# A Trainium2 encoder: the second mixer's key and query projections made pair by pair, and GpSimd scaling the softmax rows of three head pairs

## The chip, the cores and the metric

One core of a Trainium2 chip. The metric is the device time of one execution in microseconds (us), the median of several runs. TensorE is PE in the profile, VectorE DVE, ScalarE ACT, GpSimd POOL and SyncE SP.

## The reference

Two sequences of 256 tokens with 1024 channels go through two layers. Each layer is a mixer and a convolutional feed-forward, both with a residual sum and a layer norm. The first mixer is neighbourhood attention with a gated unit; the second, which the change touches, is latent attention beside a convolution branch:

```
h = x @ w_in;  c_q, c_kv, k_r, glu_a, glu_g = split(h)
q = rmsnorm(c_q) @ w_uq        # 8 heads, 64 plain + 32 rotary channels
k, v = split(rmsnorm(c_kv) @ w_ukv)
p = softmax((q . k) * 96 ** -0.5);  c = p @ v
d = glu_a * sigmoid(glu_g)
d = silu(layernorm(dwconv31(d)))
m = concat([c, d]) @ w_out
x = layernorm(ALPHA * x + m)
```

## The kernel before

All data are fp32. A large product is made of three matmuls on reduced-precision halves: a weight comes by DMA as `raw`, ACT rounds it to `whi` (L109), DVE makes the rest `wlo` (L111); activations are split in the same way (`split`, L114). PE runs 128x512 matmuls of these (`mm`, L95).

The second mixer (`odd_mixer`, L532) handles 512 tokens at once, eight heads as four pairs. `glu(i)` makes one quarter of the convolution branch's input: two products `glu` with `xT`, then a Sigmoid on ACT (L551), a product on DVE into `dpad`, and the start of that quarter's 31-tap convolution. The 21 first taps run on DVE, summing in PSUM (`cacc`, L719); the ten others are products on ACT (`pr`, L723) that GpSimd sums into `acc` (L724). They run beside the attention. `cproj` and `chain` make the normalized latents `cT`. `kvproj` makes V and the keys `kT` of all pairs, and `qproj` the queries `qT` of all pairs, both ahead of `glu(2)`.

`attend(p)` calls `attention` (L480) for a pair: for each sequence the scores of both heads go to PSUM banks `s` (two buffers), DVE takes the row maximum (L491), ACT the exponentials with their sums (L494) into a tile `er`, DVE the inverse sums `ri` (L497). Then the rows are scaled by `ri`: on ACT (L501, two instructions of 128x256) in pairs 0 to 2, on DVE (L503) in pair 3. PE transposes the result into `pt` (L508), ACT copies it to `PTr` (L510), and PE multiplies it with V (`pv`), which is split into `mixT`. The tiles `er` are a fixed ring of four. The output projection `op` (banks `op` and `dn`) takes `mixT` of the attention and then of the convolution; `conv_ln` (L727) norms the latter. GpSimd adapts the old residual (`affine`, L191). `ToFeat.done` (L228) norms a block of 128 tokens, PE transposes it (`lnT`, L237), ACT and DVE split it into the `xT` of the feed-forward (L246 to L249), whose products are `up`.

A scheduler sets the order in which each engine's instructions stand: it moves work between these steps by priorities and by its own estimate of times, so that the matmuls of `glu(2)` and `glu(3)`, say, stand among those of the attention. Semaphores hold each instruction until its operands are there and its buffer is free.

Of the kernel before, what the change touches and what calls it, by code (L numbers as in the profile page):

```python
# [11 lines left out]
AF = mybir.ActivationFunctionType  # L12
ALU = mybir.AluOpType
AX = mybir.AxisListType

P = 128
D = 1024
KC = 8
S = 256
T = 512  # L20
# [29 lines left out]
def tile_encoder(ctx: ExitStack, tc: tile.TileContext, I, O):  # L50
    nc = tc.nc
# [7 lines left out]
    pB = ctx.enter_context(tc.tile_pool(name="pB", bufs=2, space=bass.MemoryType.PSUM))  # L59
    pC = ctx.enter_context(tc.tile_pool(name="pC", bufs=2, space=bass.MemoryType.PSUM))  # L60
# [7 lines left out]
    def act(shape, dt=F32, s="a"):  # L68
        return actp.tile(shape, dt, tag="act", name=nm(s))

    def tmp(shape, dt=F32, s="t"):
        return tp.tile(shape, dt, tag="tmp", name=nm(s))
# [4 lines left out]
    class Ring:  # L77
# [6 lines left out]
        def get(self):  # L84
            j = self.i % (2 * len(self.t))
            self.i += 1
            return self.t[j // 2][:, j % 2, :].rearrange("p (a k) -> p a k", a=2)

    def bank(pool, s="ps"):
        return pool.tile([P, 512], F32, tag="b", name=nm(s))  # L90

    last_mm = [None]

    def mm(out, lhsT, rhs, first, last):
        last_mm[0] = nc.tensor.matmul(out=out, lhsT=lhsT, rhs=rhs, start=first, stop=last)  # L95
# [384 lines left out]
    def attention(p, score, V, mix, post, er, PTr, on_act=False, last_pair=False):  # L480
        for s in range(2):
            PT = [PTr.get(), PTr.get()]
            pss = [bank(pB, "s").rearrange("p (a k) -> p a k", a=2) for _ in range(2)]
            for qt in range(2):
                score([pss[h][:, qt, :] for h in range(2)], slice(s * S + qt * P, s * S + qt * P + P),
                      slice(s * S, s * S + S))
            for h in range(2):
                e = er.get()
                sc = post(pss[h], h, e)
                nmx = small(2, "nmx")  # L490
                nc.vector.tensor_reduce(out=nmx, in_=sc, axis=AX.X, op=ALU.max, negate=True)  # L491
                rs = small(2, "rs")
                for qt in range(2):
                    nc.scalar.activation(out=e[:, qt, :], in_=sc[:, qt, :], func=AF.Exp,  # L494
                                         bias=nmx[:, qt:qt + 1], accum_out=rs[:, qt:qt + 1])
                ri = small(2, "ri")
                nc.vector.reciprocal(out=ri, in_=rs)  # L497
                last_ri[0] = ri[:, 0:1]
                for qt in range(2):
                    if on_act:  # L500
                        nc.scalar.activation(out=e[:, qt, :], in_=e[:, qt, :], func=AF.Copy, scale=ri[:, qt:qt + 1])  # L501
                    else:
                        nc.vector.tensor_scalar(out=e[:, qt, :], in0=e[:, qt, :], scalar1=ri[:, qt:qt + 1],  # L503
                                                scalar2=None, op0=ALU.mult)
                pt = bank(pC, "pt")
                for kc in range(2):
                    for qt in range(2):
                        nc.tensor.transpose(pt[:, (2 * kc + qt) * P:(2 * kc + qt + 1) * P],  # L508
                                            e[:, qt, kc * P:(kc + 1) * P], ident)
                (nc.vector.tensor_copy if last_pair else nc.scalar.copy)(  # L510
                    out=PT[h], in_=pt.rearrange("p (k q) -> p k q", k=2))

            def pv_stage(s=s, PT=PT):
                pv = bank(pC, "pv")
                for kc in range(2):
                    for h in range(2):
                        mm(pv[h * 64:(h + 1) * 64, :S], V[s][:, kc, (2 * p + h) * 64:(2 * p + h + 1) * 64],
                           PT[h][:, kc, :], kc == 0, kc == 1)
                split(mix, pv[:, :S], slice(s * S, s * S + S))
            flush_pv()  # L520
            pend.append(pv_stage)
# [10 lines left out]
    def odd_mixer(xT):  # L532
# [37 lines left out]
        pr_ring = Ring(1, "pr")  # L570
        rope = const.tile([P, 2, 2, 32], F32, name="rope")
        after_mm(nc.gpsimd.dma_start(out=rope, in_=I["rope"]), last_mm[0])
        G = {"start": last_mm[0]}

        def cproj():
            psc = dn_banks()
            wc = [wload(I["wc"][:, 2 * k2:2 * k2 + 2, :].rearrange("p k n -> p (k n)"), 832) for k2 in range(4)]
            G["wkv"] = wload(I["wukv"], 1024)
            G["wq"] = [wload(I["wuq"][:, k, :], 1024) for k in range(2)]
            for s in range(2):  # L580
                for k in range(KC):
                    o = (k % 2) * 416
                    for t in (2 * s, 2 * s + 1):
                        gemm_tok([psc[t]], xT[k], t, *wc[k // 2], [slice(o, o + 416)], k == 0, k == KC - 1)
            G["psc"] = psc

        def chain():
            cT = G["cT"] = [act([P, 2, T], F32R, "cT") for _ in range(3)]
            G["kr"] = act([P, 2, T], s="kr")
            krT, ropeT = G["kr"][:, 0, :], G["kr"][:, 1, 0:S]  # L590
# [43 lines left out]
                                                                in1=cT[i][:, 0, :].bitcast(F32), op0=ALU.mult,  # L634
                                                                op1=ALU.subtract)

        def qproj():
            cT = G["cT"]
            wq = G["wq"]
            ropeT = G["kr"][:, 1:2, 0:S].broadcast_to([P, 2, S])  # L640
            qT = G["qT"] = [act([P, 2, T], s="qT") for _ in range(4)]

            def qfeat(pool, c):
                ps = bank(pool, "q")
                for k in range(2):
                    wh, wl = wq[k][0][:, c * P:(c + 1) * P], wq[k][1][:, c * P:(c + 1) * P]
                    mm(ps, wh, cT[k][:, 0, :], k == 0, False)
                    mm(ps, wh, cT[k][:, 1, :], False, False)
                    mm(ps, wl, cT[k][:, 0, :], False, k == 1)
                return ps  # L650
            for p in range(4):
                ps = qfeat(pB, 4 + p)
                for h in (0, 1):
                    rows = slice(64 - 64 * h, 128 - 64 * h)
                    nc.vector.tensor_tensor(out=qT[p][rows, h, :].rearrange("p (s t) -> p s t", s=2),  # L655
                                            in0=ps[rows].rearrange("p (s t) -> p s t", s=2), in1=ropeT[rows],
                                            op=ALU.mult)
                ps = qfeat(pC, p)
                for h in (0, 1):
                    rows = slice(64 * h, 64 * h + 64)  # L660
                    nc.scalar.activation(out=qT[p][rows, h, :], in_=ps[rows], func=AF.Copy, scale=96 ** -0.5)

        def kvproj():
            cT = G["cT"]
            wkv = G["wkv"]
            V = G["V"] = [wp.tile([P, 2, 512], F32, tag="w", name=nm("V1")) for _ in range(2)]
            for t in range(NT):
                ps = bank(pB, "v1")
                gemm_tok([ps], cT[2], t, wkv[0], wkv[1], [slice(512, 1024)], True, True)
                nc.scalar.copy(out=V[t // 2][:, t % 2, :], in_=ps)  # L670
            kT = G["kT"]
            for p in range(4):
                ps = bank(pC, "k1")
                wh, wl = wkv[0][:, p * P:(p + 1) * P], wkv[1][:, p * P:(p + 1) * P]
                mm(ps, wh, cT[2][:, 0, :], True, False)
                mm(ps, wh, cT[2][:, 1, :], False, False)
                mm(ps, wl, cT[2][:, 0, :], False, True)
                for h in range(2):
                    rows = slice(64 * h, 64 * h + 64)
                    nc.scalar.copy(out=kT[p][rows, h, :], in_=ps[rows])  # L680

        def attend(p):
            if p == 0:
                G["ring"] = Ring(2, "er"), Ring(2, "PTr")
            er, PTr = G["ring"]
            qT, kT = G["qT"][p], G["kT"][p]

            def score(out, qs, ks):
                for h in range(2):
                    mm(out[h], qT[:, h, qs], kT[:, h, ks], True, True)  # L690
            mixT[p] = act([P, 2, T], F32R, "mixT")
            if p == 2:
                G["sink"] = ToFeat(xscr[1], 1, last_mm[0], "ln1_g1", "ln1_b1", xscr[2], ())
            attention(p, score, G["V"], mixT[p], lambda ps, h, e: ps, er, PTr, p < 3, p == 3)
# [4 lines left out]
        cproj()  # L699
        chain()  # L700
        glu(1)
        kvproj()
        qproj()
        glu(2)
        attend(0)
        attend(1)
        glu(3)
        op = OutProj("wout1", mixT, [0, 1, 2, 3], [4, 5, 6, 7])
# [6 lines left out]
        for i in range(4):  # L715
            a, a2 = accps[i].rearrange("p (s t) -> p s t", s=2), acc2[i // 2][:, i % 2]
            for j in range(1, 31 - NPOOL):
                with tc.issue_after(G["cT_lo"].ins) if i == 0 and j >= 18 else nullcontext():
                    nc.vector.scalar_tensor_tensor(out=a, in0=dpad[i][:, :, j:j + S], scalar=pc("cw", i * 32 + j),  # L719
                                                   in1=a, op0=ALU.mult, op1=ALU.add)  # L720
# [201 lines left out]
```

## Time and profile before

| | us |
|---|---|
| runs | 1105.21, 1104.36, 1104.05 (median 1104.36) |
| the profiled execution | 1104.76 |
| its span | 1102.9 |
| PE busy in the span | 1082.3 (98%) |
| DVE, ACT, GpSimd busy | 673.2, 488.7, 226.6 |
| chain that ended last, share of PE | 93% |

Busy time is the time in which at least one instruction of the engine ran; an idle engine costs only where PE waits for it. The second mixer stands from about 560 to 740 us of the span.

### The profile page before, as it was taken

The page shows a single profiled execution, that of the slowest core. Times are in us where ns is not written, and L with a number is a line of the kernel's source. Part 1 is how long each engine was busy: PE and PEld are TensorE (multiplying, and loading weights), DVE is VectorE, ACT ScalarE, POOL GpSimd, SP SyncE. Part 2 cuts the span into 40 slices and gives each one's busy share as a digit, 9 for nine tenths or more (in the row PEclk, how much of TensorE's full clock was granted, in tenths as well). Part 3 has the DMA queues.
Part 4 walks back from the last instruction along what each step waited for, and adds up shares of the span by engine and source line. Part 5 has one row for each costly group of instructions (what it writes and reads, how often), then busy time and mean ns, then how long its engine had stood idle before and what let it go on. Part 6 is the DMA issues. An engine that isn't in the chain of part 4 may idle for free.

```text
span 1102.9 us, 13655 instructions
## 1 busy us (share of the span) xinstructions
PE 1082.3 (98%) x5210; PEld 900.8 (82%) x5210; DVE 673.2 (61%) x996; ACT 488.7 (44%) x783; POOL 226.6 (21%) x222
## 2 busy tenths in 40 slices
PE   9999999999999999999999979999999999999996
PEld 7888778988888888888898856899888888888885
DVE  5378955766565656422578999587665656542227
ACT  5436644544444444421266797355444444431110
POOL 0482001200000000005464661830000000000173
PEclk9999999999999999999999979999999999999999
DMA  7852223533333323645232104254333333222602
GB/s 256 244 141 77 60 103 107 163 105 96 96 96 96 96 96 99 206 166 180 80 122 58 38 20 153 66 172 122 100 96 96 96 96 96 96 96 96 215 34 76
DMA packets 36098, 124.21 MB, mean 113 GB/s; under 512 B 4289, under 2 KB 5057, under 8 KB 36033
## 3 DMA queue, kind: packets, MB, share of 16 engines
q1 hardware_dynamic: 28864, 100.05, 29.5%
q0 software_dynamic: 6448, 22.53, 6.0%
q8 instruction: 41, 0.67, 0.3%
q10 hardware_dynamic: 720, 0.75, 0.2%
q14 instruction: 25, 0.20, 0.1%
HBM read 113.88 MB, written 8.39 MB: 111 GB/s over the span
## 4 chain that ended last, share of the span: by engine, by line
PE 93%; DVE 3%; ACT 2%; issue 1%; DMA 0%; POOL 0%; POOLq 0%; DVEq 0%; ACTq 0%
PE up L95 44%; PE dn L95 29%; PE qk L95 4%; PE op L95 4%; PE glu L95 3%; PE v L95 2%; PE u L95 2%; PE s L95 1%; PE pv L95 1%; PE pt L508 1%; DVE cacc L719 1%; PE lnT L237 1%; DVE wlo L111 1%; DVE qT L655 0%; ACT er L494 0%
## 5 line engine op out<-in xcount | busy, mean ns | idle before, releaser
L95 PE MATMUL up<-xT,whi 128*128 128x512 f32 (+1 forms) x1536 | 439.9, 371 | 0.0
L111 DVE TENSOR_TENSOR wlo<-raw,whi 128x1024 fp32r<-128x1024 f32 (+1 forms) x174 | 238.8, 1374 | 297.4 <-ACT whi L109 296.1
L95 PEld LDWEIGHTS up<-xT,whi 128*128 128x128 f32 x1536 | 279.9, 188 | 49.9
L109 ACT CAST whi<-raw 128x1024 fp32r<-128x1024 f32 (+1 forms) x174 | 182.4, 1050 | 249.1 <-PE dn L95 132.6
L95 PE MATMUL up<-xT,wlo 128*128 128x512 f32 (+1 forms) x768 | 284.0, 372 | 0.0
L95 PE MATMUL dn<-whi,gT 128*128 128x512 f32 x704 | 217.4, 389 | 0.0
L95 PEld LDWEIGHTS up<-xT,wlo 128*128 128x128 f32 x768 | 144.4, 188 | 24.9
L95 PEld LDWEIGHTS dn<-whi,gT 128*128 128x128 f32 x704 | 132.0, 188 | 27.2
L95 PE MATMUL dn<-wlo,gT 128*128 128x512 f32 x352 | 136.9, 389 | 0.0
L186 POOL DMA_DIRECT2D xres<-xscr x12 | 6.5, 546 | 576.0 <-PE dn L95 576.0
L95 PEld LDWEIGHTS dn<-wlo,gT 128*128 128x128 f32 x352 | 66.1, 188 | 13.8
L115 ACT CAST gT<-cv 128x512 fp32r<-128x512 f32 x44 | 27.3, 620 | 111.6 <-DVE cv L782 111.6
L771 ACT ACTIVATE cv<-up,par 128x512 f32<-128x512 f32 x88 | 68.3, 776 | 0.0
L774 DVE SCALAR_TENSOR_TENSOR cv<-up,par,cv 128x510 f32<-128x510 f32 x88 | 65.8, 748 | 2.7
L781 ACT ACTIVATE cv<-cv 128x512 f32<-128x512 f32 x44 | 27.8, 632 | 85.2 <-DVE cv L774 85.2
L772 DVE SCALAR_TENSOR_TENSOR cv<-up,par,cv 128x510 f32<-128x510 f32 x88 | 65.4, 743 | 0.0
L719 DVE SCALAR_TENSOR_TENSOR cacc<-dpad,par,cacc 128x512 f32<-128x512 f32 x80 | 58.9, 750 | 1.1
L724 POOL TENSOR_TENSOR acc<-acc,pr 128x512 f32<-128x512 f32 x36 | 48.7, 1353 | 38.9 <-ACT pr L723 32.2
L116 DVE TENSOR_TENSOR gT<-cv,gT 128x512 fp32r<-128x512 f32 x44 | 30.4, 692 | 27.5 <-ACT gT L115 27.5
L95 PE MATMUL op<-whi,mixT 128*128 128x512 f32 x128 | 44.3, 402 | 0.0
L95 PE MATMUL dn<-whi,mixT 128*128 128x512 f32 x128 | 42.8, 394 | 0.0
L95 PE MATMUL glu<-xT,khi 128*128 128x512 f32 (+1 forms) x160 | 42.0, 349 | 0.0
(195 smaller groups left out, 1351.4 us busy)
## 6 DMA issues: line engine op xcount, KB each, us to landing
raw<-in_wup SPq DMA_DIRECT2D x88, 512.0 KB, 3.6
raw<-in_wdn SPq DMA_DIRECT2D x44, 512.0 KB, 3.5
raw<-in_wout SPq DMA_DIRECT2D x16, 512.0 KB, 3.7
xscr<-xres POOLq DMA_DIRECT2D x12, 512.0 KB, 3.7
xres<-xscr POOLq DMA_DIRECT2D x12, 512.0 KB, 4.4
raw<-in_wqk SPq DMA_DIRECT2D x8, 512.0 KB, 6.6
raw<-in_wglu SPq DMA_DIRECT2D x8, 512.0 KB, 3.8
raw<-in_wug SPq DMA_DIRECT2D x7, 512.0 KB, 3.6
```

The source lines that it names most:

```text
L95: last_mm[0] = nc.tensor.matmul(out=out, lhsT=lhsT, rhs=rhs, start=first, stop=last)
L109: nc.scalar.copy(out=hi[:, :n], in_=raw[:, :n])
L111: nc.vector.tensor_tensor(out=lo[:, :n], in0=raw[:, :n], in1=hi[:, :n].bitcast(F32), op=ALU.subtract)
L115: nc.scalar.copy(out=dst[:, 0, sl], in_=src)
L116: nc.vector.tensor_tensor(out=dst[:, 1, sl], in0=src, in1=dst[:, 0, sl].bitcast(F32), op=ALU.subtract)
L237: nc.tensor.transpose(self.banks[k // 2][:, (k % 2) * S + q * P:(k % 2) * S + q * P + P], x[:, k * P:(k + 1) * P], ident)
L719: nc.vector.scalar_tensor_tensor(out=a, in0=dpad[i][:, :, j:j + S], scalar=pc("cw", i * 32 + j), in1=a, op0=ALU.mult, op1=ALU.add)
L724: nc.gpsimd.tensor_tensor(out=a2, in0=a2, in1=pr, op=ALU.add)
L771: nc.scalar.activation(out=c, in_=pv, func=AF.Identity, scale=pc(fw, ch * 4 + 1), bias=pc(fw, ch * 4 + 3))
L772: nc.vector.scalar_tensor_tensor(out=c[:, :, 1:S], in0=pv[:, :, 0:S - 1], scalar=pc(fw, ch * 4), in1=c[:, :, 1:S], op0=ALU.mult, op1=ALU.add)
L774: nc.vector.scalar_tensor_tensor(out=c[:, :, 0:S - 1], in0=pv[:, :, 1:S], scalar=pc(fw, ch * 4 + 2), in1=c[:, :, 0:S - 1], op0=ALU.mult, o ...
L781: nc.scalar.activation(out=cg, in_=cg, func=AF.Silu)
```

## The change

`kvproj` and `qproj` become `kqproj(p)`, which makes the key, the rotary and the plain query of one pair, and `vproj`. Pairs 0 and 1 and V are made ahead of `glu(2)`, pairs 2 and 3 after `attend(0)`. In pairs 0 to 2 one GpSimd instruction of 128x512 multiplies a head's rows by `ri`, repeated along the row, in place of ACT's two. The tile `e` now comes from the pool of temporaries (eight buffers, shared with the Sigmoid's and other tiles). Lines of code move by four.

```diff
--- before.py
+++ after.py
@@ -85,6 +85,10 @@
+
+    class Loose:
+        def get(self):
+            return tmp([P, 512], s="e").rearrange("p (a k) -> p a k", a=2)
@@ -496,10 +500,10 @@
                 ri = small(2, "ri")
                 nc.vector.reciprocal(out=ri, in_=rs)
                 last_ri[0] = ri[:, 0:1]
+                if on_act:
+                    nc.gpsimd.tensor_tensor(out=e, in0=e, in1=ri[:, :, None].broadcast_to([P, 2, S]), op=ALU.mult)
                 for qt in range(2):
-                    if on_act:
-                        nc.scalar.activation(out=e[:, qt, :], in_=e[:, qt, :], func=AF.Copy, scale=ri[:, qt:qt + 1])
-                    else:
+                    if not on_act:
                         nc.vector.tensor_scalar(out=e[:, qt, :], in0=e[:, qt, :], scalar1=ri[:, qt:qt + 1],
                                                 scalar2=None, op0=ALU.mult)
@@ -634,55 +638,51 @@
+        def kqproj(p):
+            cT, wkv, kT = G["cT"], G["wkv"], G["kT"][p]
...
+            qT = G["qT"][p] = act([P, 2, T], s="qT")
+            ps = bank(pC, "k1")
...
+            for h in range(2):
+                rows = slice(64 * h, 64 * h + 64)
+                nc.scalar.copy(out=kT[rows, h, :], in_=ps[rows])
+            ps = qfeat(pB, 4 + p)
...
+            ps = qfeat(pC, p)
...
+        def vproj():
...
         def attend(p):
             if p == 0:
-                G["ring"] = Ring(2, "er"), Ring(2, "PTr")
-            er, PTr = G["ring"]
+                G["ring"] = Ring(2, "PTr")
+            er, PTr = Loose(), G["ring"]
@@ -699,10 +699,13 @@
         glu(1)
-        kvproj()
-        qproj()
+        kqproj(0)
+        kqproj(1)
+        vproj()
         glu(2)
         attend(0)
+        kqproj(2)
+        kqproj(3)
         attend(1)
         glu(3)
```

The scheduler moves more than these lines. Three places:

ACT around gate 3, where `sig` is the Sigmoid on the bank `glu` and `er` or `e` an exponential. Before:

```order
L494 ACTIVATE er_5018,rs_5050<-s_5028,nmx_5048 128x256 x2
L501 ACTIVATE er_5018<-er_5018,ri_5053 128x256 x2
L551 ACT_TABLE_LOAD
L551 ACTIVATE sig_5243<-glu_5194 128x512
L510 COPY PTr_5022<-pt_5042 128x512
L559 ACTIVATE acc_705_4425<-dpad_4421,par 128x512
L723 ACTIVATE pr_4428<-dpad_4421,par 128x512 x2
L494 ACT_TABLE_LOAD
L494 ACTIVATE er_5019,rs_5071<-s_5063,nmx_5069 128x256 x2
```

With the change:

```order
L498 ACTIVATE e_5152,rs_5155<-s_5146,nmx_5153 128x256 x2
L514 COPY PTr_4968<-pt_5133 128x512
L119 CAST mixT_4972<-pv_5139 128x256
L498 ACTIVATE e_5167,rs_5170<-s_5147,nmx_5168 128x256
L555 ACT_TABLE_LOAD
L555 ACTIVATE sig_5239<-glu_5190 128x512
L498 ACT_TABLE_LOAD
L498 ACTIVATE e_5167,rs_5170<-s_5147,nmx_5168 128x256
L514 COPY PTr_4969<-pt_5161 128x512
L107 ACTIVATE tab_5241<-sig_5239 128x1
L563 ACTIVATE acc_705_4425<-dpad_4421,par 128x512
```

The copies and convolution products that stood between the two table loads now stand behind the second; the two halves of one head's exponentials stand around the loads, and the rows with `ri` are gone from ACT.

PE at the end of the mixer, the last block of `dn` and the first `up` of the feed-forward (`xres` are the blocks of tokens). Before:

```order
L237 MATMUL lnT_5891<-ident,xres_5255 128x128 x2
L237 MATMUL lnT_5892<-ident,xres_5255 128x128 x2
L95 MATMUL dn_950_5744<-whi_5845,mixT_5640 128x512
L95 MATMUL dn_950_5744<-wlo_5847,mixT_5640 128x512
L95 MATMUL dn_950_5744<-whi_5845,mixT_5640 128x512
L95 MATMUL dn_950_5744<-whi_5851,mixT_5641 128x512
L95 MATMUL dn_950_5744<-wlo_5853,mixT_5641 128x512
L95 MATMUL dn_950_5744<-whi_5851,mixT_5641 128x512
L95 MATMUL dn_950_5744<-whi_5851,mixT_5642 128x512
L95 MATMUL dn_950_5744<-wlo_5853,mixT_5642 128x512
L95 MATMUL dn_950_5744<-whi_5851,mixT_5642 128x512
L95 MATMUL up_6109<-xT_5943,whi_6105 128x256
```

With the change:

```order
L99 MATMUL dn_964_5744<-wlo_5853,mixT_5641 128x512
L99 MATMUL dn_964_5744<-whi_5851,mixT_5641 128x512
L99 MATMUL dn_964_5744<-whi_5851,mixT_5642 128x512
L99 MATMUL dn_964_5744<-wlo_5853,mixT_5642 128x512
L241 MATMUL lnT_5889<-ident,xres_5251 128x128 x2
L241 MATMUL lnT_5890<-ident,xres_5251 128x128 x2
L241 MATMUL lnT_5891<-ident,xres_5251 128x128 x2
L241 MATMUL lnT_5892<-ident,xres_5251 128x128 x2
L99 MATMUL dn_964_5744<-whi_5851,mixT_5642 128x512
L99 MATMUL up_6109<-xT_5943,whi_6105 128x256
```

Of the nine matmuls between the last transposes and the first `up`, eight now stand ahead of the transposes.

DVE at the same place: `wlo` are halves of the feed-forward's weights, the rows with `sm` residual sums, `CAST xT` the first operand of `up`. Before:

```order
L217 TENSOR_SCALAR xres_5255<-xres_5255,sm_5252,v_5930 128x1024
L201 SCALAR_TENSOR_TENSOR xres_5257,sm_5252<-xres_5257,dn_949_5743 128x512
L212 TENSOR_SCALAR sm_5252<-sm_5252 128x1
L111 TENSOR_TENSOR wlo_6121<-raw_6117,whi_6119 128x1024
L201 SCALAR_TENSOR_TENSOR xres_5259,sm_5252<-xres_5259,op_958_5806 128x512
L111 TENSOR_TENSOR wlo_6128<-raw_6124,whi_6126 128x1024
L247 CAST xT_5943<-xv_5944 128x256
```

With the change:

```order
L221 TENSOR_SCALAR xres_5251<-xres_5251,sm_5248,v_5930 128x1024
L115 TENSOR_TENSOR wlo_6121<-raw_6117,whi_6119 128x1024
L205 SCALAR_TENSOR_TENSOR xres_5255,sm_5248<-xres_5255,op_972_5806 128x512
L115 TENSOR_TENSOR wlo_6128<-raw_6124,whi_6126 128x1024
L115 TENSOR_TENSOR wlo_6353<-raw_6349,whi_6351 128x1024
L205 SCALAR_TENSOR_TENSOR xres_5255,sm_5248<-xres_5255,dn_964_5744 128x512
L115 TENSOR_TENSOR wlo_6360<-raw_6356,whi_6358 128x1024
L251 CAST xT_5943<-xv_5944 128x256
```

Between the normalization of the second block and the first `xT` stood two sums and two halves; now two sums and four halves.

## Rows read from the trace of the kernel before

**Rows 1.** The page: busy us, share and count; TensorE clock in slices

```profile
PE 1082.3 (98%) x5210; PEld 900.8 (82%) x5210; DVE 673.2 (61%) x996; ACT 488.7 (44%) x783; POOL 226.6 (21%) x222
...
PEclk9999999999999999999999979999999999999999
```

**Rows 2.** Table of stretches: us, busy by engine (count), PE clock, DMA share, GB/s

```profile
640.00:660.00 20.00, 12.78 (x47) 8.12 (x46) 18.15 (x33) 19.31 (x44) 10.52 (x10) 0.66 0.01 1
660.00:680.00 20.00, 18.42 (x109) 12.80 (x108) 18.85 (x40) 18.89 (x57) 4.72 (x8) 1.00 0.50 184
```

**Rows 3.** PE's timeline: start us, us, engine line op out<-in count [idle before]

```profile
598.67 0.62 PE L95 MATMUL k<-cT,whi 128*128 128x512 f32 x2
...
638.54 1.02 PE L95 MATMUL s<-kT,qT 128*128 128x256 f32 x4
...
647.50 2.07 PE L95 MATMUL s<-kT,qT 128*128 128x256 f32 x4 [6.20 <-ACT er L494]
```

**Rows 4.** Table of stretches, finer

```profile
640.00:645.00 5.00, 1.30 (x9) 0.91 (x7) 3.56 (x6) 4.69 (x8) 0.50 (x2) 0.94 0.00 0
645.00:650.00 5.00, 2.13 (x5) 1.23 (x5) 4.59 (x9) 4.97 (x11) 2.48 (x3) 0.50 0.01 2
655.00:660.00 5.00, 5.00 (x25) 3.56 (x22) 5.00 (x11) 4.65 (x14) 3.01 (x4) 0.70 0.00 0
```

**Rows 5.** ACT's timeline around gate 3

```profile
640.51 1.28 ACT L551 ACT_TABLE_LOAD   x1
641.81 0.60 ACT L551 ACTIVATE sig<-glu 128x512 f32<-128x512 f32 x1
...
645.13 1.28 ACT L494 ACT_TABLE_LOAD   x1
```

**Rows 6.** Groups by line, 560 to 820 us: count, busy us, mean ns

```profile
L724 POOL TENSOR_TENSOR acc<-acc,pr 128x512 f32<-128x512 f32 x36 | 48.7, 1353 | 38.9 <-ACT pr L723 32.2 <-issue 4.9
...
L494 ACT ACTIVATE er<-s,nmx 128x256 f32<-128x256 f32 x32 | 14.9, 476 | 4.2 <-DVE nmx L491 4.1
...
L501 ACT ACTIVATE er<-er,ri 128x256 f32<-128x256 f32 x24 | 11.1, 510 | 0.2 <-DVE ri L497 0.2
L491 DVE TENSOR_REDUCE nmx<-s 128x2 f32<-128x512 f32 x16 | 10.8, 672 | 0.0
...
L494 ACT ACTIVATION_READ_ACCUMULATOR er<-s,nmx 128x1 f32 x32 | 6.6, 206 | 0.0
```

**Rows 7.** Groups by line, GpSimd, whole span

```profile
L403 POOL TENSOR_TENSOR bias<-bias,mask 128x1024 f32<-128x1024 f32 x4 | 9.5, 2396 | 0.1
```

**Rows 8.** Timelines of DVE and GpSimd where weight halves meet sums

```profile
629.66 3.81 DVE L111 TENSOR_TENSOR wlo<-raw,whi 128x1024 fp32r<-128x1024 f32 x2
...
630.44 4.17 POOL L724 TENSOR_TENSOR acc<-acc,pr 128x512 f32<-128x512 f32 x2 [0.27 <-ACT pr L723]
```

**Rows 9.** PE's timeline at the seam to the feed-forward

```profile
728.61 1.03 PE L237 MATMUL lnT<-ident,xres 128*128 128x128 f32 x8
729.40 0.48 PE L95 MATMUL dn<-whi,mixT 128*128 128x512 f32 x1
...
731.31 0.39 PE L95 MATMUL dn<-whi,mixT 128*128 128x512 f32 x1
731.54 0.64 PE L95 MATMUL up<-xT,whi 128*128 128x256 f32 x4
```

**Rows 10.** DVE's timeline at the same place

```profile
728.35 0.69 DVE L201 SCALAR_TENSOR_TENSOR xres<-xres,op 128x512 f32<-128x512 f32 x1 [0.17 <-PE op L95]
...
729.20 1.22 DVE L111 TENSOR_TENSOR wlo<-raw,whi 128x1024 fp32r<-128x1024 f32 x1 [0.16 <-ACT whi L109]
730.34 0.69 DVE L247 CAST xT<-xv 128x256 fp32r<-128x256 f32 x3
```

**Rows 11.** GpSimd's timeline, affine of the residual

```profile
690.36 10.41 POOL L194 TENSOR_TENSOR xres<-xres,rowg 128x1024 f32<-128x1024 f32 x4
```

More of the change, by code (lines that the diff above doesn't have):

```diff
@@ L572, in odd_mixer @@
         after_mm(nc.gpsimd.dma_start(out=rope, in_=I["rope"]), last_mm[0])
-        G = {"start": last_mm[0]}
+        G = {"start": last_mm[0], "qT": [None] * 4}
         def cproj():
@@ L635, in chain @@
                                                                 op1=ALU.subtract)
-        def qproj():
-            cT = G["cT"]
-            wq = G["wq"]
-            ropeT = G["kr"][:, 1:2, 0:S].broadcast_to([P, 2, S])
[L641 to L661, printed above, removed]
@@ L663, in kvproj, with qfeat @@
-        def kvproj():
-            cT = G["cT"]
-            wkv = G["wkv"]
+        def qfeat(pool, c):
+            cT, wq = G["cT"], G["wq"]
+            ps = bank(pool, "q")
+            for k in range(2):
+                wh, wl = wq[k][0][:, c * P:(c + 1) * P], wq[k][1][:, c * P:(c + 1) * P]
+                mm(ps, wh, cT[k][:, 0, :], k == 0, False)
+                mm(ps, wh, cT[k][:, 1, :], False, False)
+                mm(ps, wl, cT[k][:, 0, :], False, k == 1)
+            return ps
+        def kqproj(p):
+            cT, wkv, kT = G["cT"], G["wkv"], G["kT"][p]
+            ropeT = G["kr"][:, 1:2, 0:S].broadcast_to([P, 2, S])
+            qT = G["qT"][p] = act([P, 2, T], s="qT")
+            ps = bank(pC, "k1")
+            wh, wl = wkv[0][:, p * P:(p + 1) * P], wkv[1][:, p * P:(p + 1) * P]
+            mm(ps, wh, cT[2][:, 0, :], True, False)
+            mm(ps, wh, cT[2][:, 1, :], False, False)
+            mm(ps, wl, cT[2][:, 0, :], False, True)
+            for h in range(2):
+                rows = slice(64 * h, 64 * h + 64)
+                nc.scalar.copy(out=kT[rows, h, :], in_=ps[rows])
+            ps = qfeat(pB, 4 + p)
+            for h in (0, 1):
+                rows = slice(64 - 64 * h, 128 - 64 * h)
+                nc.vector.tensor_tensor(out=qT[rows, h, :].rearrange("p (s t) -> p s t", s=2),
+                                        in0=ps[rows].rearrange("p (s t) -> p s t", s=2), in1=ropeT[rows],
+                                        op=ALU.mult)
+            ps = qfeat(pC, p)
+            for h in (0, 1):
+                rows = slice(64 * h, 64 * h + 64)
+                nc.scalar.activation(out=qT[rows, h, :], in_=ps[rows], func=AF.Copy, scale=96 ** -0.5)
@@ L666, in kvproj @@
+        def vproj():
+            cT, wkv = G["cT"], G["wkv"]
             V = G["V"] = [wp.tile([P, 2, 512], F32, tag="w", name=nm("V1")) for _ in range(2)]
@@ L670, in kvproj @@
                 nc.scalar.copy(out=V[t // 2][:, t % 2, :], in_=ps)
[L671 to L680, printed above, removed]
         def attend(p):
             if p == 0:
-                G["ring"] = Ring(2, "er"), Ring(2, "PTr")
-            er, PTr = G["ring"]
+                G["ring"] = Ring(2, "PTr")
+            er, PTr = Loose(), G["ring"]
             qT, kT = G["qT"][p], G["kT"][p]
```

## The prediction

> **What bounds the kernel now.** I read the page's busy line and clock line first [rows 1]: TensorE (PE) is busy 98% of 1102.9 us, at full clock but for one hole past the middle of the span. So the end moves only by what PE waits, or by what it runs at half clock; the other engines count only through that. The table of stretches puts the hole into the attention of the second mixer [rows 2]: 640 to 660 us has 12.78 of 20 us of PE at a mean clock of 0.66, 660 to 680 has 18.42, while ScalarE (ACT) has 19.31 and 18.89 and VectorE (DVE) 18.15 and 18.85. There two engines that elsewhere hide behind PE are full, and PE waits for them.
>
> PE's timeline shows the hole itself [rows 3]: the score product that takes 1.02 us at 638.5 takes 2.07 us at 647.5, after 6.20 us of waiting for ACT's exponentials. [...] ACT's timeline says what held the scores [rows 5]: gate 3's Sigmoid needs another function table than the exponentials, so a load of 1.28 us, the Sigmoid (0.60), a copy and three convolution products, and a second load of 1.28 us stand between two exponentials.
>
> **The sum is made against** the profiled execution: 1104.76 us for the run, 1102.9 of it the span, 0.4 us above the median of 1104.36.
>
> **The change, part by part.** The projections are the same matmuls in another order, so PE's own work is unchanged; what can change is how long PE waits. ACT loses 24 multiplications of 510 ns in pairs 0 to 2, 11.1 us busy, and GpSimd gets 12 multiplications of 128x512 instead [rows 6]. The two memsets of the removed ring are off every path. DVE keeps its own scaling in pair 3. SP's queue keeps its order; on GpSimd's queue six DMA issues (residual and affine rows) now stand behind a softmax multiplication, but what they bring is first used at 690 us [rows 11], some 30 us later, so I cost that at nothing; were it late, the affine's 22 us would start late by as much.
>
> The price of one GpSimd multiplication is not in the trace. The nearest row is its own convolution sum, the same shape and type in the same stretch, 1353 ns [rows 6]; the mask sum over 128x1024 with a broadcast operand takes 2396 ns [rows 7], which is 1.2 us for half the size. I take 1.35, the nearest, with 1.2 as the low end; the high end is twice the broadcast row, 2.4, should a scalar repeated along a row be slow. [...]
>
> One more price: the low half of a weight (128x1024 on DVE) takes 1.22 us alone [rows 10], but two of them took 3.81 us while GpSimd summed, and two of GpSimd's sums 4.17 instead of 2.7 [rows 8]. Where the two meet I let one wait for the other.
>
> *Attention.* I laid the new order of all engines out row by row, from the first key projection to the first up-projection, each instruction starting when its engine is free and its operands are done, with the rows' durations at full clock. The old order laid out in the same way needs 131.6 us where the trace has 132.9 (598.67 to 731.54 [rows 3, 9]), and has 6.5 us for the long wait where the trace has 6.20, so the method is good to about 1 us; most of the missing 1.3, some 1.1, is what the half clock cost on the path. In the new order the long wait shrinks: ACT has one exponential, load, Sigmoid, load, the next exponential, with nothing else between the loads. 1.28 + 0.60 + 1.28 and that exponential with its readout (0.7) are 3.9 us [rows 5, 6]; PE still has four transposes, and waits about 3.0 where it waited 6.2. **But the gain is spent** in smaller waits. With the product on GpSimd a head goes through row maximum 0.67, two exponentials with readouts 1.3 and product 1.35, where ACT's two products took 1.0 [rows 6]; and in pair 0 each product can queue behind a convolution sum (1.35). By my layout transposes in pairs 0 and 1 wait 1.2, 1.3 and 0.9 us for GpSimd and a score 1.6 us for ACT; in pairs 2 and 3 scores wait 1.5 and 1.1, output matmuls 1.0 and 0.9, and one output matmul 1.8 us for the convolution's share. Waits over 0.25 us add up to 15.9 us in the old order and to 16.0 in the new. Term: 0.0.
>
> *Seam to the last feed-forward.* Here the order of the tail moves, as the pieces in the section on the change show. Today, after the second group of lnT transposes (728.61), PE has nine matmuls, 2.1 us (729.40 to 731.54 [rows 9]), while ACT and DVE make the first xT; its cast starts at 730.34 and the first up-projection at 731.54 without a wait [rows 9, 10]. In the new order one matmul stands there, and DVE has four weight halves and two residual sums between the second normalization and the first cast: 4 x 1.14 (start to start) + 2 x 0.69 + 0.3 = 6.2 us [rows 10]. PE has 8 matmuls of 0.23 and 16 transposes, eight in 0.79, in that time [rows 9]: 3.4 us. It waits the difference and a hand-over, about 3.1; at least 2.2, because the last residual sum needs PE's last matmul and is followed by a half (1.22) and the cast. Late next: four up matmuls run, then the low half of xT, which stands behind four casts that ACT feeds one by one: 1.0 us. Then the transposes of the second sequence, whose normalization follows all that: 0.9. Together 5.0; the old order, laid out, has 0.6. Term: **+4.4 us**.
>
> *Clock.* With no wait over about 3 us I take it that the clock stays up, which gives back 1.1 us. Whether a wait of 3.0 us is short enough the trace cannot say: the clock fell 3 us into one of 6.2. If it falls, the stretch 650 to 664 has four or five scores, each 1.04 us longer in its head's chain [rows 3]: from nothing to +4 instead of -1.1.
>
> Sum: 0.0 + 4.4 - 1.1 = **+3.3 us**; with 1.2 us per product +2.7, with 1.5 +4.2. On the median, 1104.4 + 3.3 = 1107.7.
>
> **The rivals.** *Relief (faster).* ACT is the fullest engine [rows 2], and 11.1 us of its work go away. If GpSimd's products end before ACT would have come to its own, only the gate's 3.0 us, the convolution's 1.8 and a few tenths of the 16 remain: -11 + 4.4 - 1.1 = -7.7, 1096.7. It decides on GpSimd's lag: with a product done within 1.0 us of the sums it wins, at 1.35 it doesn't. For it speak ACT's rows; against it that DVE is as full [rows 2] and keeps every maximum and convolution tap. 0.12.
> *Even.* The seam's waits are partly taken back because a longer attention leaves the weights of the tail ready earlier, or moving the products does nothing that PE notices: within 0.2% of 1104.4, that is 2.2 us, about what a measurement of this kernel can tell from no change. 0.21.
> *Clock falls in the attention.* 4.4 + about 2 = +6.4, 1110.8. 0.22.
> *Slow product.* At 2.4 us ten or so products on PE's path are 1.05 us longer each: +3.3 + 10, 1118. Against it: the broadcast row was no slower per element than the plain one [rows 6, 7]. 0.06.
>
> **How the numbers follow.** The forecast has 0.39. Slower by over 0.2%: 0.39 + 0.22 + 0.06 = 0.67; within: 0.21; faster: 0.12. The range leaves out relief and the slow product, 0.18 in all; it reaches down over the even case (1104.4 - 1.9) and up over a fallen clock with a product of 1.5 us and 1 us for the layout (6.4 + 0.9 + 1): 1102.5 to 1113.0.
>
> **What would show it.** Right: no wait of PE over 3.5 us in the attention; pt transposes released by GpSimd; a wait of 2.2 to 3.5 us before the first up-projection, released by the cast; granted clock 1.0 from 600 to 740. Wrong: a first up-projection without a wait (the seam term falls), a GpSimd product far from 1.35 us, or a stretch from the first key projection to the first up-projection, 132.9 now, outside 133 to 138.

## The result: 1.2% slower, and the profile after

The changed kernel takes 1117.16 us (1116.10 to 1119.40, four runs) against 1104.32 for the kernel before: a ratio of 1.0118, interval 1.0100 to 1.0135, or 12.8 us. The forecast was +3.3 and its range ended at 1113.0. The profiled execution took 1117.68 us. Its page, span, busy line and clock line, which answer to [rows 1]:

```profile
span 1115.9 us, 13650 instructions
## 1 busy us (share of the span) xinstructions
PE 1086.8 (97%) x5210; PEld 904.2 (81%) x5210; DVE 674.5 (60%) x994; ACT 480.5 (43%) x759; POOL 236.6 (21%) x234
...
PEclk9999999999999999999999989999999999999999
```

ACT has lost 8.2 us of work and GpSimd got 10.0. PE does the same 5210 matmuls in 4.5 us more (1086.8 - 1082.3), and stands idle 29.1 us instead of 20.6. So 8.5 of the 13.0 us by which the span grew are waits, and in 4.5 the same matmuls take longer, mostly at a lower clock: at half clock (granted clock 0.50) PE was busy 9.7 us before and 17.1 now, and half of the difference, 3.7 us, is an estimate of what that cost. The table of stretches (columns as in [rows 2]) shows that the hole is no longer in one place:

```profile
640.00:660.00 20.00, 13.21 (x57) 9.46 (x58) 14.09 (x24) 16.66 (x36) 3.32 (x4) 0.91 0.37 106
660.00:680.00 20.00, 17.22 (x85) 12.63 (x83) 17.89 (x37) 15.45 (x44) 15.34 (x17) 0.91 0.43 157
680.00:700.00 20.00, 17.17 (x91) 12.06 (x90) 17.79 (x30) 6.55 (x14) 5.23 (x6) 0.91 0.10 28
700.00:720.00 20.00, 18.13 (x85) 14.78 (x84) 11.59 (x14) 7.10 (x10) 17.03 (x8) 0.91 0.26 78
740.00:760.00 20.00, 17.80 (x135) 17.60 (x136) 11.30 (x32) 9.51 (x20) 10.76 (x12) 0.91 0.36 132
```

From 640 to 660 PE does even a little more than before, and at a better clock. The loss lies behind it. Five stretches, this one among them, have a mean clock of 0.91, where the kernel before had one of 0.66 and then 1.00. In finer stretches each is one dip of 3.4 us to a granted clock of 0.50, at 650.8, 661.0, 684.9, 708.8 and 742.9. The waits ahead of them, in PE's timeline (columns as in [rows 3]), with the first key projection at the top:

```profile
598.50 0.62 PE L99 MATMUL k<-cT,whi 128*128 128x512 f32 x2
...
650.65 2.00 PE L99 MATMUL s<-kT,qT 128*128 128x256 f32 x4 [2.31 <-ACT e L498]
...
659.57 1.13 PE L99 MATMUL s<-kT,qT 128*128 128x256 f32 x4 [3.22 <-ACT e L498]
...
683.51 0.50 PE L99 MATMUL dn<-whi,mixT 128*128 128x512 f32 x1 [2.36 <-ACT e L498]
...
707.90 0.50 PE L99 MATMUL op<-whi,mixT 128*128 128x512 f32 x1 [1.87 <-ACT mixT L119]
...
741.88 0.74 PE L99 MATMUL up<-xT,whi 128*128 128x256 f32 x4 [2.13 <-DVE xT L251]
```

From the first key projection to the first up-projection it is 143.4 us, where it was 132.9. The wait of 3.22 us is gate 3's, which was 6.20 [rows 3]. ACT's timeline there answers to [rows 5]:

```profile
655.18 0.48 ACT L498 ACTIVATE e<-s,nmx 128x256 f32<-128x256 f32 x1
...
655.75 1.28 ACT L555 ACT_TABLE_LOAD   x1
657.05 0.60 ACT L555 ACTIVATE sig<-glu 128x512 f32<-128x512 f32 x1
657.66 1.28 ACT L498 ACT_TABLE_LOAD   x1
658.96 0.47 ACT L498 ACTIVATE e<-s,nmx 128x256 f32<-128x256 f32 x1
```

Nothing stands between the two loads, as forecast. But the Sigmoid starts at 657.05 and started at 641.81, although its product was done at 635.8, 2.9 us earlier than in the kernel before (638.7). The last quarter of the convolution hangs on it: its 21 taps on DVE end 15 us later (690.0, before 675.1), its nine sums on GpSimd start 17 us later (661.4, before 644.6) and end 26 us later (686.8, before 661.0), and both run into the fourth pair. DVE's scalings of that pair:

```profile
674.71 0.91 DVE L507 TENSOR_SCALAR e<-e,ri 128x256 f32<-128x256 f32 x2
...
677.51 0.60 DVE L507 TENSOR_SCALAR e<-e,ri 128x256 f32<-128x256 f32 x2
...
679.75 2.05 DVE L507 TENSOR_SCALAR e<-e,ri 128x256 f32<-128x256 f32 x2
...
684.89 2.10 DVE L507 TENSOR_SCALAR e<-e,ri 128x256 f32<-128x256 f32 x2
```

and GpSimd's sums and the affine of the residual at the same time:

```profile
679.02 2.63 POOL L727 TENSOR_TENSOR acc<-acc,pr 128x512 f32<-128x512 f32 x2 [3.82 <-ACT pr L726]
684.21 2.63 POOL L727 TENSOR_TENSOR acc<-acc,pr 128x512 f32<-128x512 f32 x2 [2.56 <-ACT pr L726]
...
704.01 11.38 POOL L198 TENSOR_TENSOR xres<-xres,rowg 128x1024 f32<-128x1024 f32 x4
```

Two scalings take 0.60 us alone, 2.05 and 2.10 beside sums, and 0.91 where the end of a sum (672.58 to 675.20) meets them; in the kernel before the sums had ended at 661.0 and all four took 0.6. The row maximum and the exponentials for which PE waits 2.36 us stand behind the first of the two slow ones. The affine comes at 704.01, not 690.36 [rows 11]. The product on GpSimd itself is cheaper than I took it (line, operation, count, then busy us and mean ns):

```profile
L504 POOL TENSOR_TENSOR e<-e,ri 128x512 f32<-128x512 f32 x12 | 12.5, 1042 | 18.5 <-DVE ri L501 18.4
```

### The profile page after: what moved, and what is told of

It is laid out like the page before. It is cut to its first block, busy times and chain, and to the rows that moved or that the text cites. A ratio compares the mean times of both kernels' runs of the same rounds, so it can differ in the third digit from the quotient of the medians.

```text
span 1115.9 us, 13650 instructions
## 1 busy us (share of the span) xinstructions
PE 1086.8 (97%) x5210; PEld 904.2 (81%) x5210; DVE 674.5 (60%) x994; ACT 480.5 (43%) x759; POOL 236.6 (21%) x234
## 4 chain that ended last, share of the span: by engine, by line
PE 93%; DVE 3%; ACT 2%; issue 1%; DMA 0%; POOL 0%; POOLq 0%; DVEq 0%; ACTq 0%
PE up L99 43%; PE dn L99 28%; PE qk L99 4%; PE op L99 4%; PE glu L99 4%; PE v L99 2%; PE u L99 2%; PE s L99 1%; DVE cacc L722 1%; PE pv L99 1%; PE pt L512 1%; PE lnT L241 1%; PE q L99 1%; DVE wlo L115 0%; ACT e L498 0%
```

## The experiments

Three things changed at once: the order of the projections (O), the product on GpSimd (G), and the tiles of the exponentials, which moved from a ring of their own to the pool of temporaries (T). I had costed the last at two memsets. The first four runs take each alone, and T away from the whole. Three dots stand for lines of the code that are not shown; the class `Loose` goes where the ring comes back, and comes where the ring goes.

**Only the order (e1).** Against the changed kernel:

```diff
-                if on_act:
-                    nc.gpsimd.tensor_tensor(out=e, in0=e, in1=ri[:, :, None].broadcast_to([P, 2, S]), op=ALU.mult)
                 for qt in range(2):
-                    if not on_act:
+                    if on_act:
+                        nc.scalar.activation(out=e[:, qt, :], in_=e[:, qt, :], func=AF.Copy, scale=ri[:, qt:qt + 1])
+                    else:
...
-                G["ring"] = Ring(2, "PTr")
-            er, PTr = Loose(), G["ring"]
+                G["ring"] = Ring(2, "er"), Ring(2, "PTr")
+            er, PTr = G["ring"]
```

> Only the projections are made pair by pair; ACT still scales the rows of pairs 0 to 2 and the exponentials keep their ring of four tiles. Theory O (the projections of pairs 2 and 3 bring their copies and casts into the attention, in front of exponentials): most of the loss is here, 1111 us or more, and the clock falls three times or more in the attention. Theory T (the exponentials' tiles, now from the pool of temporaries, are what costs) and theory G (the product on GpSimd, by its lag and by what it does to DVE): within 3 us of the kernel before, and a first up-projection that waits under 0.5 us.

Measured: 1103.89 us, ratio 0.9997 (0.9988 to 1.0005). The order costs nothing; theory O falls. The wait of 6.20 us is split up, the longest is 1.71, and there is one dip to half clock, of 6.8 us. In the table of stretches the two that hold the attention read:

```profile
640.00:660.00 20.00, 14.20 (x61) 9.05 (x59) 19.04 (x29) 19.46 (x37) 12.53 (x9) 0.92 0.20 55
660.00:680.00 20.00, 18.39 (x100) 12.73 (x97) 18.93 (x41) 18.37 (x58) 4.19 (x9) 0.91 0.58 210
```

**Only the product on GpSimd (e2).** The kernel before, with

```diff
+                if on_act:
+                    nc.gpsimd.tensor_tensor(out=e, in0=e, in1=ri[:, :, None].broadcast_to([P, 2, S]), op=ALU.mult)
                 for qt in range(2):
-                    if on_act:
-                        nc.scalar.activation(out=e[:, qt, :], in_=e[:, qt, :], func=AF.Copy, scale=ri[:, qt:qt + 1])
-                    else:
+                    if not on_act:
```

> Only the scaling of pairs 0 to 2 goes to GpSimd; projections and ring as before. Theory G: 1110 us or more, with DVE's scalings in pair 3 above 600 ns on average. Theories O and T: within 3 us of the kernel before; a product of 1.04 us in place of two of 510 ns costs next to nothing.

Measured: 1106.17 us, ratio 1.0018 (1.0010 to 1.0027): 2 us, neither nothing nor the loss. DVE's scalings in pair 3 take 0.6 us for two as before; GpSimd's sums end at 661.2 there.

**Only the tiles (e3).** The kernel before, with

```diff
-                G["ring"] = Ring(2, "er"), Ring(2, "PTr")
-            er, PTr = G["ring"]
+                G["ring"] = Ring(2, "PTr")
+            er, PTr = Loose(), G["ring"]
```

> Only the exponentials' tiles come from the pool of temporaries; ACT scales, projections as before. Theory T: 1110 us or more, with the affine of the residual starting after 700 us, a wait of over 1.5 us before the first up-projection and one of over 1.5 us for the convolution's share in the output projection. Theories O and G: within 3 us of the kernel before, no such waits.

Measured: 1114.26 us, ratio 1.0094 (1.0080 to 1.0107). An edit that changes no arithmetic costs 10 us. The affine starts at 701.7, the first up-projection waits 2.13 us, the convolution's share 1.86, all as theory T had them. ACT's timeline shows the same place for the Sigmoid as in the changed kernel, between the two halves of one exponential:

```profile
654.72 0.47 ACT L498 ACTIVATE e<-s,nmx 128x256 f32<-128x256 f32 x1
...
655.27 1.28 ACT L555 ACT_TABLE_LOAD   x1
656.57 0.60 ACT L555 ACTIVATE sig<-glu 128x512 f32<-128x512 f32 x1
657.18 1.28 ACT L498 ACT_TABLE_LOAD   x1
658.48 0.47 ACT L498 ACTIVATE e<-s,nmx 128x256 f32<-128x256 f32 x1
```

**The change without the tiles (e4).** The changed kernel, with the edit of e3 the other way round.

> The whole change but with the ring of four tiles. Theory T: 1104 to 1109 us, the first up-projection without a wait of over 0.5 us and no wait for the convolution's share. Theories O and G: within 3 us of the changed kernel (1114 to 1120).

Measured: 1108.36 us, ratio 1.0031 (1.0019 to 1.0042). So T holds most of the loss. The 4 us that stay come with the product's move to GpSimd, on top of an order that costs nothing by itself. The two longest waits in its timeline of PE are

```profile
656.41 2.08 PE L99 MATMUL s<-kT,qT 128*128 128x256 f32 x4 [4.21 <-ACT er L498]
660.90 1.11 PE L512 MATMUL pt<-ident,er 128*128 128x128 f32 x4 [2.42 <-POOL er L504]
```

The longer one is not at gate 3, whose Sigmoid stands at 637.75 here, and it is hardly new: it is for exponentials behind other work on ACT, around which e1 has waits of 1.46 and 1.71 us. New is the wait for GpSimd; all waits over 0.25 us ahead of the seam add up to 11.7 us here and to 8.7 in e1. GpSimd's timeline says why the transposes wait 2.42 us: a convolution sum, and then two products, of 3.04 us together:

```profile
657.59 1.27 POOL L727 TENSOR_TENSOR acc<-acc,pr 128x512 f32<-128x512 f32 x1 [1.81 <-ACT pr L726]
658.82 3.04 POOL L504 TENSOR_TENSOR er<-er,ri 128x512 f32<-128x512 f32 x2
```

The first of the two took 2.02 us, where the median is 1.04. DVE made the low half of a weight beside it:

```profile
658.70 1.24 DVE L115 TENSOR_TENSOR wlo<-raw,whi 128x1024 fp32r<-128x1024 f32 x1
```

**Why do tiles cost time?** Gate 3's Sigmoid also writes a tile of that pool, and `glu(3)` follows `attend(1)` in the program. In both kernels with the moved tiles it stands right behind the first half of that pair's last exponential. Theory Q: the pool hands out its buffers in the order of the program, so the scheduler cannot place the Sigmoid until the pair's last tile `e` has its own, however early its operand is there. Theory T2: the tail's temporaries (of the norm and the feed-forward), which share the pool too, are what ties it. Two edits tell them apart; e5 gives the Sigmoid its own buffer, e6 only exchanges lines of the program:

```diff
-            sg = tmp([P, 512], s="sig")
+            sg = sp.tile([P, 512], F32, tag="sig", bufs=1, name=nm("sig"))
```

> The whole change, and the Sigmoid's tile of each gate comes from a buffer of its own instead of the pool of temporaries that the exponentials now use. Theory Q (buffers of one pool are handed out in the order of the program, so gate 3's Sigmoid, which follows the second pair in the program, cannot stand ahead of that pair's last exponential; its convolution is then 15 to 20 us late): the Sigmoid of gate 3 starts at 636 to 643 us, the affine before 695 us, the first up-projection waits under 0.5 us, and the time is that of the change with the ring kept, 1106 to 1110 us. Theory T2 (it is other temporaries that share the pool, of the norm and of the feed-forward, that tie the tail): the tail stays as in the changed kernel, 1113 us or more.

```diff
         kqproj(3)
+        glu(3)
         attend(1)
-        glu(3)
```

> The whole change with two lines exchanged: the third gate's products and gate stand in the program ahead of the second pair's attention, pool and tiles unchanged. Theory Q: Sigmoid of gate 3 before 645 us, 1106 to 1111 us. Theory T2: 1113 us or more, with the affine after 700 us.

Measured: e5 1107.82 us, ratio 1.0036 (1.0024 to 1.0049); e6 1108.32, 1.0034 (1.0022 to 1.0047). In both the Sigmoid starts at 637.7, the affine at 691, and the first up-projection has no wait of over 0.25 us. Theory Q stands: 9 of the 13 us are the place of one Sigmoid. Both runs leave the ring out, so that what the ring did elsewhere, by the memory it held, is not the cause. ACT's timeline of e5:

```profile
636.47 1.28 ACT L555 ACT_TABLE_LOAD   x1
637.76 0.60 ACT L555 ACTIVATE sig<-glu 128x512 f32<-128x512 f32 x1
```

**Order and pool, Sigmoid freed, ACT scaling (e7).** e5 with the first half of e1's diff.

> Projections pair by pair, exponentials' tiles from the pool of temporaries, Sigmoid's tile with a buffer of its own, but ACT scales the rows as before. Theory Q: 1103 to 1106 us, as with the new order of the projections alone, since pool and order then cost nothing. Theory T2: 1111 us or more.

Measured: 1104.74 us, ratio 1.0005 (0.9996 to 1.0014). Pool and order are free together; the step from here to e5, 3 us, comes with GpSimd's product again.

**The clock (e8).** Theory C was that a wait of some 2 us lowers the clock (the five dips above stand behind 1.87 to 3.22 us) and that a dip costs up to 1.7 us beyond the wait, half of its 3.4 us. With the clock held up behind the seam the time would then fall by 1 to 2 us, to 1115 to 1116, and the first up-projection start when it did. The changed kernel, with

```diff
         head = [load(0), load(1)]
+        if l == 1:
+            for _ in range(16):
+                mm(head[0][0][0][:, 0:256], warm[:, 0:P], warm, True, True)
```

> The changed kernel, with sixteen small matmuls on zeros (1.7 us in all) put on TensorE ahead of the first up-projection, into the bank that this then overwrites; they add nothing to the result. [...] Rival (the half clock only fills time in which TensorE would wait for the next operands): the dip goes, the time stays within 0.5 us or rises.

Measured: 1115.62 us (1115.56 to 1117.44), ratio to the kernel before 1.0107 (1.0093 to 1.0121). PE's timeline at the seam:

```profile
737.68 0.48 PE L99 MATMUL dn<-whi,mixT 128*128 128x512 f32 x1
738.00 1.92 PE L99 MATMUL up<-warm 128*128 128x256 bf16 x16
740.29 0.75 PE L99 MATMUL up<-xT,whi 128*128 128x256 f32 x4 [0.37 <-DVE xT L251]
...
743.75 0.39 PE L99 MATMUL up<-xT,whi 128*128 128x256 f32 x1 [0.71 <-POOL xT L253]
```

The first up-projection starts 2.61 us after the last `dn`, to the hundredth as in the changed kernel (739.27 to 741.88). The table of stretches has no dip, where the changed kernel has 0.73, 0.50 and 0.92 from 742 on:

```profile
740.00:742.00 2.00, 1.39 (x9) 1.19 (x10) 2.00 (x11) 2.00 (x5) 1.35 (x1) 1.00 1.00 383
742.00:744.00 2.00, 1.29 (x11) 1.09 (x11) 1.18 (x6) 1.20 (x3) 2.00 (x2) 1.00 0.60 231
744.00:746.00 2.00, 2.00 (x19) 2.00 (x18) 0.15 (x1) 0.97 (x2) 2.00 (x4) 1.00 0.01 2
```

But from the first up-projection to the end it gained only 0.5 us (1115.9 - 741.88 = 374.0 against 1113.8 - 740.29 = 373.5): PE came sooner to an operand of GpSimd's that was not there, the 0.71 us above. The total lies in theory C's range, but not by its means; the rival was mostly right at the seam. The other 1.6 us of the two traces come from ahead of the seam, where the edit adds nothing: this run has two dips there (651.2, 671.7) and the changed kernel's had four, with nearly the same waits. So a dip cost 0.5 to 0.8 us of time in these two executions, an estimate, less than the 1.7 us of matmul work (half of 3.4) that it can take. It may also cost nothing: two executions of e8 with mean clocks of 0.995 and 0.992, a difference of some two dips, took 1115.59 and 1115.56.

**A version without the loads.** sigmoid(g) = (1 + tanh(g/2))/2, and in ACT's timeline of e10, at the end of this section, no load of a table stands between an exponential and the tangent (starts at 635.47 and 635.93), where a load of 1.28 us stands ahead of the Sigmoid in the kernel before [rows 5]. Gates 2 and 3 become

```diff
-            nc.scalar.activation(out=sg, in_=pg, func=AF.Sigmoid)
...
-            nc.vector.tensor_tensor(out=out, in0=va, in1=vs, op=ALU.mult)
...
+                nc.scalar.activation(out=sg, in_=pg, func=AF.Tanh, scale=0.5)
+                nc.vector.scalar_tensor_tensor(out=out, in0=vs, scalar=1.0, in1=va, op0=ALU.add, op1=ALU.mult)
```

with the taps of those quarters halved once at the start, and the exponentials' table loaded behind gate 1. On the kernel before (e9), on the new order of e1 (e10), on e5 (e11), and on e10 with DVE scaling pair 2 too, `p < 2` in place of `p < 3` (e12):

> The kernel before, with the gates of the third and fourth quarter made of a hyperbolic tangent: sigmoid(g) = (1 + tanh(g/2))/2, the half taken into the taps of those two quarters. The tangent is in the table of the exponentials, so that ACT loads no table at gate 3. Theory G3 (the wait of 6.20 us at 641 is the two loads and what stands between them): the wait falls to 3.5 us or less, the clock's long dip of 13.65 us is shorter by a third or more, 1100 to 1103 us. Rival (the next bound, DVE and ACT full, takes the place): the wait is split up and the time stays within 1 us of the kernel before.

> The new order of the projections alone (ring kept, ACT scales) with the tangent in gates 2 and 3. If the loads are worth something in this order too: 1100 to 1102 us, faster than both kernels; if ACT's other work is the bound there, 1103 to 1105 as without it.

> The whole change with a buffer of its own for the Sigmoid and the tangent in gates 2 and 3: what the products on GpSimd cost when neither the gate's place nor its tables hold the attention. If the cost lies in GpSimd's queue (a product behind a convolution sum, and the transposes behind the product): 1103 to 1107 us, 2 to 4 above the run with the new order and the tangent. If it lay at the gate: no difference from that run.

> The new order with the tangent, and DVE scales the rows of pair 2 as well as of pair 3 (0.6 us for a head in place of 1.02 on ACT). If ACT is the bound in pair 2: 1 to 2 us below the run with the new order and the tangent. If DVE is: the same or slower.

Measured: e9 1103.13 us, ratio 0.9988 (0.9979 to 0.9997): the wait of 6.20 is 3.29 and the dip 10.2 us, a quarter shorter, not a third, and the time just above the forecast's 1103. e10 1101.08, 0.9970 (0.9958 to 0.9981), the fastest of all and ahead of both kernels: no wait over 1.71 us and a dip of 6.8. e11 1104.13, 0.9997 (0.9988 to 1.0005): 3 us above e10, so GpSimd's cost does not lie at the gate. Waits for GpSimd are there, 0.71 and 1.44 us of transposes, but of the 3.5 us between the spans of e10 and e11 only 1.3 are idle time and 2.2 are longer matmuls (PE busy 1083.4 against 1081.2), with dips of 10.2 and 3.4 us against one of 6.8. e12 1102.74, 0.9987 (0.9978 to 0.9996): slower than e10, and its transposes in pair 2 wait 0.44, 0.42 and 1.02 us for DVE; DVE has no room there either. ACT at gate 3 in e10:

```profile
635.47 0.48 ACT L494 ACTIVATE er<-s,nmx 128x256 f32<-128x256 f32 x1
...
635.93 0.60 ACT L557 ACTIVATE sig<-glu 128x512 f32<-128x512 f32 x1
636.41 0.60 ACT L510 COPY PTr<-pt 128x512 f32<-128x512 f32 x1
```

## Why the prediction was wrong

**The step that failed** is the attention's term of 0.0, and with it the clock's of -1.1. Waits over 0.25 us ahead of the seam grew from 8.7 to 14.3 us, by 5.6, and the same matmuls took 4.5 us longer: +10.1 where the two terms had -1.1. The stretch from the first key projection to the first up-projection took 143.4 us, far outside the 133 to 138 that I had named. That the kernel became slower, as forecast, is in part luck: the forecast had it from the seam, and the seam is the smallest of the three.

What stands behind these terms is the step that took the removed ring for two memsets off every path. The tiles' move cost 9 to 10 us: 1.0094 alone (e3), and 1.0118 with it in the whole change against 1.0031 with the ring kept (e4) and 1.0036 with the Sigmoid freed (e5). The 3 to 4 us that are left came with the product. I had the new place of the Sigmoid in front of me, between the halves of an exponential, and read from it only that the wait at the gate shrinks. I did not compare its time with the old one, and of what comes behind it, one quarter of the convolution 15 us late, the prediction has only the wait for the convolution's share.

**The gate's wait**: forecast 3.0 us, measured 3.22. Right, but the other waits ahead of the seam grew from 2.5 to 11.1 us.

**The smaller waits**: the convolution's share was forecast at 1.8 and is 1.87. Of the three waits of transposes for GpSimd (1.2, 1.3, 0.9) there is one, 1.02. All waits over 0.25 us ahead of the seam add up to 14.3 us where I had 16.0. But for the old order my layout had 15.9, and the trace has 8.7, in part because PE spent some of that time on matmuls at half clock. I compared the layouts' waits and saw the total agree within 1 us; the kernel before really stood at 8.7, so these waits were worth +5.6, not 0.0. The layout, with the rows' durations, also had 0.6 us for two scalings of pair 3 where they took 2.05 and 2.10 beside sums (0.60 without): GpSimd's neighbour on DVE was to be looked at after the move, not only the weight halves [rows 8]. Why they are slow beside a sum, no run shows.

**The product**: 1.042 us, not 1.35; the row of a sum was too dear a neighbour. By the relief rival a product near 1.0 us should have won; it lost 2 us in the old order and 3 to 4 in the new (e2, e4, e7 to e5, e10 to e11). Its length alone does not decide. What stands ahead of it on GpSimd and beside it on DVE counts too: in e4 transposes waited 2.42 us for a product that stood behind a sum (1.27) and took 2.02 beside a weight's half on DVE. Nor is it all waiting, as the busy times of e10 and e11 show. How the 3 us divide among the queue, DVE and the clock stays open; GpSimd without the convolution's sums was not tried.

**The seam**: the place was right, a wait for the cast and one for its low half, and the sign. The size was 2.13 and 0.32 us, and no third wait, for 3.1, 1.0 and 0.9: +2.5 for +4.4. And it is no effect of its own: with the Sigmoid early it is gone (e4, e5, e6).

**The clock**: that it stays up with no wait over about 3 us was an estimate from one fall, at about 644.4 by the mean of 0.94 [rows 4], 3.1 us into the wait of 6.20 us [rows 3]. It was wrong. Five dips stood behind waits of 1.87 to 3.22 us. The rival with a fallen clock had one fall and about +2; at 0.5 to 0.8 us each, the estimate of e8, five are 2.5 to 4.0 us, and the 1.1 that I took as given back was not.

## What to carry to other kernels

Before costing a tile's new pool at nothing, ask which other tiles take their buffers from it, and which of them the scheduler had moved ahead of its place in the program: the move may bind it there again. When an instruction changes place, date it on both sides and follow what it feeds to the end, even if the wait at its own place gets shorter. And when a layout is tried out on the old kernel, compare it wait by wait: a total can agree because two errors cancel.

## What the runs showed of the hardware that I had not expected

Waits of 1.87 us (at 706.0) and 2.13 us (at 739.8) were followed by half clock in the changed kernel, yet in e8 the same wait of 1.87 us, one of 2.36 and one of 3.22 us were not, and a dip at 671.7 had only waits of 1.19 and 0.76 us ahead of it: the length of a wait alone does not decide it. The changed kernel's runs spread over 3.3 us, those of the kernel before over 1.2, and the mean clocks of its four runs roughly go with their times: 0.993 and 0.992 for 1116.64 and 1116.10 us, 0.990 for 1117.68, 0.987 for 1119.40. So the dips differ from run to run; that they make the spread would fit, but only one execution of each kernel has a trace.

On GpSimd a product with a scalar repeated along the row took 1.04 us for 128x512, and a plain sum of two tiles of that size 1.31 (the changed kernel) to 1.35 [rows 6], means of 36; a single one between two products took 1.28 (the changed kernel, at 627.51).
